# Placing the index chain in TensorE's order, laying the PSUM banks of two layers otherwise, and one square sum on VectorE

## The chip, the cores and the metric

The kernel runs on one core of a Trainium2 chip. The metric is the device time of one execution in microseconds (us). A core has a matrix engine (TensorE, in the profile PE, with its weight loads as PEld), VectorE (DVE), ScalarE (ACT), GpSimd (POOL) and SyncE (SP), which here issues transfers. TensorE writes its results into PSUM, which the kernel uses as eight banks of 128 partitions by 512 fp32 numbers.

## The reference

A decoder trunk of two layers over 512 positions of width 1024, all in fp32. Cut to what matters here:

```python
def rmsnorm(x, g):
    y = x * rsqrt(mean(x * x, axis=-1) + EPS)
    return y * g

def even_layer(x, ...):                      # layer 0
    p = rmsnorm(x, g_norm) @ w_in            # q, k, v, o, z_a, gates, u, z_b
    y_a = mLSTM(conv(q), conv(k), v, gates)  # 4 heads of 256, output gate, head norm, silu gate
    y_b = multi-scale causal pooling of u    # 4 groups, silu gate
    return x + concat(y_a, y_b) @ w_out

def odd_layer(x, ...):                       # layer 1
    p = rmsnorm(x, g_norm) @ w_in            # q, ckv, qi, ki, wi, z
    k, v = rmsnorm(ckv) @ w_uk, rmsnorm(ckv) @ w_uv      # 16 heads of 64, q and k normed
    for each block of 128 queries:
        score = sum over 4 index heads of wi * relu(qi . ki)     # causal
        idx   = top_k(score, 128)                                # min(256, 512 // 4)
        out   = softmax(q . k[idx] / 8 + bias) @ v[idx]
    return x + (out * silu(z)) @ w_out
```

## The kernel before

**Products.** Every fp32 product is done as three fp32r matmuls: an operand is split into a rounded part `h` and a rest `l`, and h*h, h*l and l*h are summed in PSUM. Activations are split by `split` (ScalarE copies `h`, L115; VectorE subtracts, L112). Weights come in tiles of at most 1024 columns (`wtile`): a transfer into `raw`, ScalarE casts `wh` (L147), VectorE or GpSimd subtracts for `wl` (L148). Each of the three has three buffers, so a fourth weight tile waits until the matmuls of the first are done. `dense_tok` (matmuls L180 to L182) gives results with tokens on the partitions, one block `t` of 128 tokens per accumulator; `dense_ch` and `part_ch` (L209 to L211) give channels on the partitions.

**Order.** The work of each stage is written as a string of steps (`ORDER_B`, `ORDER_A` for layer 0, `ORDER` for layer 1), run one after the other; a scheduler then simulates the engines and sets the final order of each engine's instructions by priority and readiness. So an instruction's place on an engine is fixed before the run, and moves when anything near it changes.

**PSUM.** `psum_pools` lays the pools onto the banks in the order of its arguments. Layer 0 has `mm` (4 banks, 0 to 3, dense accumulators) and `bg` (4 banks, 4 to 7, all else). Layer 1 has `mm` (3 banks, 0 to 2), `qk` (2 banks, 3 and 4, query-key products), `tr` (2 banks, 5 and 6, transposes) and `po` (1 bank, 7). `bg()` gives a `tr` bank in layer 1.

**Start.** While x arrives in eight pieces, `arrive(k)` scales it by the norm's gain and `squares(k)` adds its squares to `ssum` (ScalarE squares, GpSimd adds, L251). `norm_factors` sums `ssum` over the channels by four matmuls with one column (L257), VectorE adds epsilon (`n_ss`, L259), GpSimd raises to -1/2 (L260, the factors `r4`), VectorE lays them on a diagonal (L262, `n_dg`), one more matmul spreads them over the partitions (L265), and ScalarE copies this to `r_bc` (L266). `v0_gates` and `tok_v_raw` scale the values of two heads by `r4` (VectorE's `v_l` is L374), `gate_chain` begins (`nf` L387, `lf` L390), and `normalise` makes the normed x: VectorE multiplies (`sq`, L313), ScalarE casts `xn_h` (L314), VectorE and GpSimd in turn subtract for `xn_l` (L315). Then the pooling steps begin with `dense_ch` on it.

**Change of layer.** The output projection of layer 0 ends in `next_x` for each of eight channel blocks: VectorE adds to `xT` (L606), `scaled` makes `xn_h` and `xn_l` (L241, L242), `squares` adds to `ssum`. `norm_factors` follows, then the pools of layer 1 are opened.

**Index stage.** A `dense_tok` with groups of one token block each gives 324 columns of the index projection (qi, ki, wi) in 24 matmuls per block t0 to t3. `ev_idx` scales the block by `r4` on ScalarE (L640 to L642), TensorE transposes it in three pieces (L645) into a `tr` bank, and `split` makes the tiles `aq` and `ak`. Then `scores` (step i, L711 to L718) forms the index scores with `head_pairs` (L679 and L682, into `qk`) and VectorE's L718; `select` (step s) takes the top 128 by rounds of max and match_replace on VectorE (L725, L726); `attend` (step a) does logits (VectorE L832, which writes `st`), the exponential and its scaling on ScalarE (L834, L836), transposes on TensorE (L844) and the products with v (L853 to L855, into `po`), and VectorE multiplies into `zy` (L859). Steps q, k, v, z are projections that fill TensorE between; `head_norm` evacuates q and k (`q_n`, L763, transposed in L767), z's evacuation is L803.

Of the kernel before, what the change touches and what calls it, by code (L numbers as in the profile page):

```python
# [12 lines left out]
ALU = mybir.AluOpType  # L13
# [4 lines left out]
NT = 4  # L18
NK = 8
# [38 lines left out]
def trunk(ctx: ExitStack, tc: tile.TileContext, a: dict, out: bass.AP):  # L58
    nc = tc.nc
    V, A, G, T = nc.vector, nc.scalar, nc.gpsimd, nc.tensor  # L60
# [5 lines left out]
    ps = {}  # L66
    ps_pools = ExitStack()

    def psum_pools(**banks):
        ps_pools.close()  # L70
        ps.clear()
        for n, b in banks.items():
            ps[n] = ps_pools.enter_context(tc.tile_pool(name="ps_" + n, bufs=b, space=PSUM))

    ctx.callback(ps_pools.close)
    psum_pools(mm=4, bg=4)

    def bank(n):
        return ps[n].tile([128, 512], F32, name=n)

    def mm():
        return bank("mm")
    dr = ctx.enter_context(tc.tile_pool(name="dr", bufs=1, space=bass.MemoryType.DRAM))

    def bg():
        return bank("bg" if "bg" in ps else "tr")
# [3 lines left out]
    ident = cst[:, O_IDENT:O_IDENT + 128]  # L90
# [20 lines left out]
    def sub_f32r(dst, src, h):  # L111
        V.tensor_tensor(dst, src, h.bitcast(F32), op=ALU.subtract)  # L112

    def split(h, l, src):
        A.copy(h, src)  # L115
        sub_f32r(l, src, h)
# [17 lines left out]
    def wtile(shape, loads, queue=nc.sync):  # L134
        n = math.prod(shape)
        raw = wp.tile([128, 1024], F32, name="raw", bufs=3)
        wh = wp.tile([128, 1024], F32R, name="wh")
        wl = wp.tile([128, 1024], F32R, name="wl")

        def view(t):  # L140
            t = t[:, :n]
            if len(shape) == 2:
                t = t.rearrange("p (x y) -> p x y", x=shape[0])
            return t
        for sl, src in loads:
            queue.dma_start(view(raw)[:, sl[0], sl[1]], src)
        A.copy(wh[:, :n], raw[:, :n])  # L147
        low_engine[0].tensor_tensor(wl[:, :n], raw[:, :n], wh[:, :n].bitcast(F32), op=ALU.subtract)  # L148
        return view(wh), view(wl)
# [3 lines left out]
    def wrows(w, r0, nk, c0, n):  # L153
        return w[r0:r0 + 128 * nk, c0:c0 + n].rearrange("(k p) c -> p k c", p=128)

    def wcols(cols, kk, queue=nc.sync):
        loads, off = [], 0
        for w, c0, m in cols:
            loads.append(((ALL, slice(off, off + m)), wrows(w, 128 * kk[0], len(kk), c0, m)))
            off += m  # L160
        return wtile([len(kk), off], loads, queue)

    def dense_tok(act, ks, cols, evac, groups=(range(NT),), share=False):

        n = sum(x[2] for x in cols)
        step = min(1024 // n, len(ks))
        ws = {}

        def part(t, k0, ps):
            kk = ks[k0:k0 + step]
            if k0 not in ws:
                ws[k0] = wcols(cols, kk)
            wh, wl = ws[k0]
            for j, k in enumerate(kk):
                ah, al = act(k)
                ts = slice(128 * t, 128 * t + 128)
                first, last = (k0 + j == 0), (k0 + j == len(ks) - 1)
                T.matmul(ps, ah[:, ts], wh[:, j], start=first, stop=False)  # L180
                T.matmul(ps, ah[:, ts], wl[:, j], start=False, stop=False)  # L181
                T.matmul(ps, al[:, ts], wh[:, j], start=False, stop=last)  # L182

        for tts in groups:
            if share:
                two = mm().rearrange("p (u c) -> p u c", u=2)
                for u, t in enumerate(tts):
                    for k0 in range(0, len(ks), step):
                        part(t, k0, two[:, u])
                evac(tts[0], two)  # L190
                continue
            acc = {t: mm() for t in tts}
            for k0 in range(0, len(ks), step):
                for t in tts:
                    part(t, k0, acc[t][:, :n])
                    if k0 + step >= len(ks):
                        evac(t, acc[t])

    def dense_ch(act, w, c0, evac, r0=0):

        ps = mm()
        part_ch(act, wtile([NK, 128], [((ALL, ALL), wrows(w, r0, NK, c0, 128))]), range(NK), ps)
        evac(ps)
# [25 lines left out]
    xn_h = per.tile([128, NK, S], F32R, name="xn_h")  # L229
    xn_l = per.tile([128, NK, S], F32R, name="xn_l")  # L230
    xn = lambda k: (xn_h[:, k], xn_l[:, k])
    ones = nm.tile([128, 128], F32, name="ones")
    V.memset(ones, 1.0)
    ssum = nm.tile([128, S], F32, name="ssum")
# [9 lines left out]
    def squares(k):  # L244

        if k == 0:
            A.activation(ssum, xT[:, k], AF.Square, scale=1.0 / 32)
            return
        sq = nm.tile([128, S], F32, name="sq", bufs=2)
        A.activation(sq, xT[:, k], AF.Square, scale=1.0 / 32)  # L250
        G.tensor_tensor(ssum, ssum, sq, op=ALU.add)  # L251

    def norm_factors():

        p = bg()
        for t in range(NT):
            T.matmul(p[:, t:t + 1], ssum[:, 128 * t:128 * t + 128], ones[:, 0:1], start=True, stop=True)  # L257
        ss = sm.tile([128, NT], F32, name="n_ss")
        V.tensor_scalar(ss, p[:, 0:NT], EPS, None, op0=ALU.add)  # L259
        G.tensor_tensor(r4, ss, mhalf[:, :NT], op=ALU.pow)  # L260
        dg = nm.tile([128, NT, 128], F32, name="n_dg", tag="sq", bufs=2)
        V.tensor_tensor(dg, ident[:, None, :].to_broadcast([128, NT, 128]),  # L262
                        r4[:, :, None].to_broadcast([128, NT, 128]), op=ALU.mult)
        p = bg()
        T.matmul(p, ones, dg.rearrange("p t c -> p (t c)"), start=True, stop=True)  # L265
        A.copy(r_bc, p)  # L266


    warm = nm.tile([128, S], mybir.dt.bfloat16, name="warm")
# [9 lines left out]
    def arrive(k):  # L279
        nc.sync.dma_start(xT[:, k], xv[:, k])  # L280
        if k == 0:
            nc.sync.dma_start(e_g, a["e_norm"])
        scaled(y_h[:, k], y_l[:, k], k, e_g)
        squares(k)

    arrive(0)
    for k in range(NK):
        low_engine[0] = V if k % 2 == 0 else G
        wh, wl = wcols([(a["e_w_in"], 2048, 256), (a["e_w_in"], 5120, 264)], [k], nc.scalar if k < 2 else nc.sync)
        wh, wl = wh[:, 0], wl[:, 0]  # L290
# [9 lines left out]
        for t in range(NT):  # L300
            ts = slice(128 * t, 128 * t + 128)
# [35 lines left out]
    w_in, w_out = a["e_w_in"], a["e_w_out"]  # L337
# [267 lines left out]
    def next_x(c, ps):  # L605
        V.tensor_tensor(xT[:, c], ps, xT[:, c], op=ALU.add)  # L606
        nc.sync.dma_start(x_one[c], xT[:, c])
        scaled(xn_h[:, c], xn_l[:, c], c, o_g)
        squares(c)

    dense_ch4(y, w_out, 0, next_x, lambda c: mm())
    for c in range(4, NK):
        dense_ch(y, w_out, 128 * c, lambda ps: next_x(c, ps))
    norm_factors()
    V.tensor_scalar(r16, r4, 1.0 / 16, None, op0=ALU.mult)

    y_pool.close()

    w_in, w_out = a["o_w_in"], a["o_w_out"]
    w_uk, w_uv = a["o_w_uk"], a["o_w_uv"]  # L620
    psum_pools(mm=3, qk=1, tr=2, po=1)
    GR = ((0, 1), (2, 3))
    p2 = ctx.enter_context(tc.tile_pool(name="p2", bufs=1))
    zy = p2.tile([128, 8, S], F32, name="zy")
# [9 lines left out]
    ki_h, ki_l = (p2.tile([128, S], F32R, name=n, tag=n, bufs=3) for n in ("ak_h", "ak_l"))  # L634
    wi = p1.tile([128, NT, 4], F32, name="wi")

    def ev_idx(t, ps):
        qk = t1.tile([128, 6, 64], F32, name="qk_tok", tag="cb")
        r = r4[:, t:t + 1]
        A.activation(qk[:, 0:5], ps[:, 0:320].rearrange("p (h c) -> p h c", h=5), AF.Copy, scale=r)  # L640
        A.copy(qk[:, 5], qk[:, 4])
        A.activation(wi[:, t], ps[:, 320:324], AF.Copy, scale=r16[:, t:t + 1])  # L642
        p = bg()[:, 0:384].rearrange("p (c t) -> p c t", c=3)
        for c in range(3):
            T.transpose(p[:, c], qk[:, 2 * c:2 * c + 2], ident)  # L645
        ts = slice(128 * t, 128 * t + 128)
        split(qi_h[:, :, ts], qi_l[:, :, ts], p[:, 0:2])
        split(ki_h[:, ts], ki_l[:, ts], p[:, 2])
    low_engine[0] = G
    dense_tok(xn, range(NK), [(w_in, 1280, 324)], ev_idx, [(t,) for t in range(NT)])  # L650


    ckv_h = p1.tile([128, 2, S], F32R, name="ckv_h")
# [261 lines left out]
```

## Time and profile before

Three runs took 760.47, 760.7 and 761.76 us, median 760.7. The profiled execution took 760.41 us, with a span from first to last instruction of 758.6 us and a mean granted TensorE clock of 0.997 of full speed.

| engine | busy us | share of the span |
|---|---|---|
| PE (matmul) | 733.3 | 97% |
| PEld (weight load, beside PE) | 621.4 | 82% |
| DVE | 458.2 | 60% |
| ACT | 383.8 | 51% |
| POOL | 304.2 | 40% |

An engine's busy time counts its instructions alone. "idle before, releaser" is the time an engine stood still ahead of an instruction and the instruction that ended the wait. Times of day are microseconds from the start of the span. The profile shows every engine's rows with their line in the kernel; names are the program's, with buffer numbers left out.

### The profile page before, as it was taken

To read this page: it belongs to the slowest core of one execution; us is meant where nothing else is said; L and a number is where in the kernel's file an instruction comes from. 1 tells how busy PE (TensorE), PEld (TensorE's weight loads), DVE (VectorE), ACT (ScalarE), POOL (GpSimd) and SP (SyncE) were. 2 spreads that over 40 slices of the span, in tenths; PEclk is the share of its full clock that TensorE was granted. 3 is DMA by queue.
4 is the path that set the end of the run, shared out by engine and by line. 5 is a ranking of instruction groups with operands and counts; after the bars stand their busy time and mean duration, and the time that the engine had idled before them with its cause. 6 is when DMAs were issued, how large, how long until landed. Compare 5 with 4: busy or idle time off the path is not lost.

```text
span 758.6 us, 11075 instructions
## 1 busy us (share of the span) xinstructions
PE 733.3 (97%) x4123; PEld 621.4 (82%) x4123; DVE 458.2 (60%) x944; ACT 383.8 (51%) x724; POOL 304.2 (40%) x254
## 2 busy tenths in 40 slices
PE   8989999999999999999999999999999998999987
PEld 6887888887888889888988888988898996777776
DVE  6686533434635866235514573399999986788531
ACT  6445333272535544344633453453565775998710
POOL 5455547723002011031363376246234752753321
PEclk9999999999999999999999999999999999999999
DMA  7623342345231323333322143513331220110061
GB/s 223 166 71 86 84 111 70 111 124 153 83 96 59 91 90 88 92 91 93 84 84 84 56 152 114 140 42 88 94 98 57 65 89 29 57 57 1 13 210 55
DMA packets 83989, 69.19 MB, mean 91 GB/s; under 512 B 3884, under 2 KB 71900, under 8 KB 83936
## 3 DMA queue, kind: packets, MB, share of 16 engines
q1 hardware_dynamic: 82144, 65.83, 30.2%
q10 hardware_dynamic: 1760, 2.66, 1.0%
q8 instruction: 32, 0.52, 0.3%
q14 instruction: 21, 0.17, 0.1%
q0 software_dynamic: 32, 0.01, 0.0%
HBM read 64.25 MB, written 4.23 MB: 90 GB/s over the span
## 4 chain that ended last, share of the span: by engine, by line
PE 79%; DVE 12%; ACT 5%; issue 2%; POOL 1%; DMA 1%; SPq 0%; DVEq 0%; POOLq 0%; ACTq 0%
PE mm L209 13%; PE mm L210 13%; PE mm L211 13%; PE mm L180 7%; PE mm L181 7%; PE mm L182 7%; DVE sel L726 1%; ACT lg L834 1%; DVE m L725 1%; DVE sel L718 1%; DVE pt_l L112 1%; PE qk L209 1%; ACT wh L147 1%; PE qk L211 1%; DVE wl L148 1%
## 5 line engine op out<-in xcount | busy, mean ns | idle before, releaser
L148 POOL TENSOR_TENSOR wl<-raw,wh 128x1024 fp32r<-128x1024 f32 (+4 forms) x65 | 148.5, 2285 | 265.0 <-ACT wh L147 220.8
L147 ACT CAST wh<-raw 128x1024 fp32r<-128x1024 f32 (+4 forms) x117 | 113.5, 972 | 175.5 <-PE mm L210 54.4
L209 PE MATMUL mm<-xn_h,wh 128*128 128x512 f32 x336 | 132.5, 396 | 4.4 <-DVE v_l L374 1.9
L210 PE MATMUL mm<-xn_l,wh 128*128 128x512 f32 x336 | 132.3, 394 | 0.0
L211 PE MATMUL mm<-xn_h,wl 128*128 128x512 f32 x336 | 131.9, 392 | 0.0
L182 PE MATMUL mm<-wh,xn_l 128*128 128x256 f32 (+2 forms) x384 | 123.6, 323 | 0.0
L181 PE MATMUL mm<-wl,xn_h 128*128 128x256 f32 (+2 forms) x384 | 123.5, 322 | 0.0
L180 PE MATMUL mm<-wh,xn_h 128*128 128x256 f32 (+2 forms) x384 | 120.8, 323 | 0.9 <-DVE xT L606 0.9
L148 DVE TENSOR_TENSOR wl<-raw,wh 128x1024 fp32r<-128x1024 f32 (+2 forms) x52 | 65.8, 1266 | 63.0 <-ACT wh L147 62.9
L180 PEld LDWEIGHTS mm<-wh,xn_h 128*128 128x128 f32 x384 | 72.0, 188 | 8.3 <-ACT wh L147 1.3
L209 PEld LDWEIGHTS mm<-xn_h,wh 128*128 128x128 f32 x336 | 63.1, 188 | 18.3 <-DVE v_l L374 2.0
L182 PEld LDWEIGHTS mm<-wh,xn_l 128*128 128x128 f32 x384 | 72.2, 188 | 6.4 <-issue 0.6
L181 PEld LDWEIGHTS mm<-wl,xn_h 128*128 128x128 f32 x384 | 72.2, 188 | 6.3 <-issue 0.5
L210 PEld LDWEIGHTS mm<-xn_l,wh 128*128 128x128 f32 x336 | 63.3, 188 | 14.1 <-issue 0.6
L211 PEld LDWEIGHTS mm<-xn_h,wl 128*128 128x128 f32 x336 | 63.2, 188 | 13.9
L211 PE MATMUL mm<-y_h,wl 128*128 128x512 f32 x128 | 50.2, 394 | 0.4 <-DVE wl L148 0.4
L210 PE MATMUL mm<-y_l,wh 128*128 128x512 f32 x128 | 50.3, 393 | 0.0
L209 PE MATMUL mm<-y_h,wh 128*128 128x512 f32 x128 | 48.8, 394 | 0.9 <-ACT y_h L115 0.9
L515 DVE SCALAR_TENSOR_TENSOR cv<-mm,s_conv,cv 128x511 f32<-128x511 f32 (+2 forms) x48 | 35.8, 746 | 16.2 <-ACT cv L513 15.3
L124 POOL TENSOR_TENSOR q_r<-q_ss,mhalf 128x8 f32<-128x8 f32 x16 | 27.2, 1701 | 40.5 <-DVE q_ss L121 32.7
L834 ACT ACTIVATE lg<-lg,st 128x128 f32<-128x128 f32 (+3 forms) x64 | 35.8, 561 | 9.4 <-DVE st L832 9.3
L836 ACT ACTIVATE lg<-lg,st 128x128 f32<-128x128 f32 (+3 forms) x64 | 34.0, 560 | 4.1 <-DVE st L835 3.9
(274 smaller groups left out, 1529.0 us busy)
## 6 DMA issues: line engine op xcount, KB each, us to landing
raw<-in_e_w_in_dram SPq DMA_DIRECT2D x52, 512.0 KB, 3.8
raw<-in_o_w_in_dram SPq DMA_DIRECT2D x18, 512.0 KB, 3.9
raw<-in_e_w_out_dram SPq DMA_DIRECT2D x16, 512.0 KB, 3.7
raw<-in_o_w_out_dram SPq DMA_DIRECT2D x8, 512.0 KB, 3.5
xT<-in_xT_dram SPq DMA_DIRECT2D x8, 256.0 KB, 3.7
x_one<-xT SPq DMA_DIRECT2D x8, 256.0 KB, 2.7
abias<-lines SPq DMA_DIRECT2D x4, 512.0 KB, 3.9
o_sb<-x_one SPq DMA_DIRECT2D x8, 256.0 KB, 4.0
```

Source lines behind the costliest of these rows:

```text
L124: G.tensor_tensor(dst, ss, mhalf[:, :n], op=ALU.pow)
L147: A.copy(wh[:, :n], raw[:, :n])
L148: low_engine[0].tensor_tensor(wl[:, :n], raw[:, :n], wh[:, :n].bitcast(F32), op=ALU.subtract)
L180: T.matmul(ps, ah[:, ts], wh[:, j], start=first, stop=False)
L181: T.matmul(ps, ah[:, ts], wl[:, j], start=False, stop=False)
L182: T.matmul(ps, al[:, ts], wh[:, j], start=False, stop=last)
L209: T.matmul(ps, wh[:, j], ah, start=(k == 0), stop=False)
L210: T.matmul(ps, wh[:, j], al, start=False, stop=False)
L211: T.matmul(ps, wl[:, j], ah, start=False, stop=(k == NK - 1))
L515: V.scalar_tensor_tensor(u[:, j:], ps[:, :S - j], w[:, 3 - j:4 - j], u[:, j:], op0=ALU.mult, op1=ALU.add)
L834: A.activation(lg[:, :n], lg[:, :n], AF.Exp, scale=-1.0, bias=st[:, 0:1], accum_out=st[:, 1:2])
L836: A.activation(lg[:, :n], lg[:, :n], AF.Copy, scale=st[:, 2:3])
```

## The change

It has four parts.

1. In layer 0 the pool `bg` is laid onto banks 0 to 3 and `mm` onto banks 4 to 7.
2. The last of the eight additions to `ssum` (k = 7), in both layers, is issued on VectorE instead of GpSimd.
3. At the change of layer `psum_pools` is called ahead of `norm_factors`, so that its matmuls write `tr` banks of layer 1; `norm_factors` returns the last of its four sum matmuls.
4. The index projection no longer goes through `dense_tok` but is written out, with three calls per token block (k0 = 0, 3, 6), and `tc.issue_after` puts four of the twelve calls behind a given instruction in TensorE's order: the start of t1 behind the norm sums, the last part of t1 behind the transposes of t0, the middle of t2 behind those of t1, the middle of t3 behind those of t2. The matmuls, evacuations and transposes are the same in number and shape.

```diff
-    psum_pools(mm=4, bg=4)
+    psum_pools(bg=4, mm=4)
...
-        G.tensor_tensor(ssum, ssum, sq, op=ALU.add)
+        (V if k == NK - 1 else G).tensor_tensor(ssum, ssum, sq, op=ALU.add)
...
-            T.matmul(p[:, t:t + 1], ssum[:, 128 * t:128 * t + 128], ones[:, 0:1], start=True, stop=True)
+            sums = T.matmul(p[:, t:t + 1], ssum[:, 128 * t:128 * t + 128], ones[:, 0:1], start=True, stop=True)
...
+        return sums
...
-    norm_factors()
+    psum_pools(mm=3, qk=1, tr=2, po=1)
+    sums = norm_factors()
...
-    psum_pools(mm=3, qk=1, tr=2, po=1)
...
-    def ev_idx(t, ps):
+    idx_acc, idx_tr = {}, {}
+
+    def idx_part(t, k0):
+
+        kk = range(k0, min(k0 + 3, NK))
+        if k0 not in idx_w:
+            idx_w[k0] = wcols([(w_in, 1280, 324)], kk)
+        wh, wl = idx_w[k0]
+        ps, ts = idx_acc[t][:, :324], slice(128 * t, 128 * t + 128)
+        for j, k in enumerate(kk):
+            T.matmul(ps, xn_h[:, k, ts], wh[:, j], start=(k == 0), stop=False)
+            T.matmul(ps, xn_h[:, k, ts], wl[:, j], start=False, stop=False)
+            T.matmul(ps, xn_l[:, k, ts], wh[:, j], start=False, stop=(k == NK - 1))
+
+    def idx_evac(t):
+        ps = idx_acc[t]
...
-            T.transpose(p[:, c], qk[:, 2 * c:2 * c + 2], ident)
+            idx_tr[t] = T.transpose(p[:, c], qk[:, 2 * c:2 * c + 2], ident)
...
-    dense_tok(xn, range(NK), [(w_in, 1280, 324)], ev_idx, [(t,) for t in range(NT)])
+    idx_w = {}
+    for t in range(NT):
+        idx_acc[t] = mm()
+        for k0 in (0, 3, 6):
+            behind = {(1, 0): sums, (1, 6): idx_tr.get(0), (2, 3): idx_tr.get(1), (3, 3): idx_tr.get(2)}.get((t, k0))
+            with tc.issue_after(behind.ins) if behind else ExitStack():
+                idx_part(t, k0)
+        idx_evac(t)
```

Below, rows of an engine's order as the scheduler left it. They hold no times.

**VectorE at the start.** Before, between the value rest `v_l` of accumulator mm_108 and that of mm_441 (a PSUM bank that the first pooling projection takes next):

```order
L374 SCALAR_TENSOR_TENSOR v_l_386<-mm_108,r4_89,v_h_385 128x256
L315 TENSOR_TENSOR xn_l_85<-sq_409,xn_h_84 128x512
L313 SCALAR_TENSOR_TENSOR sq_417<-xT_83,e_g_104,r_bc_91 128x512
L390 SCALAR_TENSOR_TENSOR lf_565<-gt_393,nf_564 128x16
L315 TENSOR_TENSOR xn_l_85<-sq_417,xn_h_84 128x512
L313 SCALAR_TENSOR_TENSOR sq_421<-xT_83,e_g_104,r_bc_91 128x512
L313 SCALAR_TENSOR_TENSOR sq_425<-xT_83,e_g_104,r_bc_91 128x512
L148 TENSOR_TENSOR wl_678<-raw_676,wh_677 128x1024
L313 SCALAR_TENSOR_TENSOR sq_429<-xT_83,e_g_104,r_bc_91 128x512
L315 TENSOR_TENSOR xn_l_85<-sq_425,xn_h_84 128x512
L374 SCALAR_TENSOR_TENSOR v_l_386<-mm_441,r4_89,v_h_385 128x256
```

After, the same place (all lines behind L73 are one or more higher):

```order
L388 SCALAR_TENSOR_TENSOR nf_564<-gt_393 128x16
L316 TENSOR_TENSOR xn_l_85<-sq_409,xn_h_84 128x512
L314 SCALAR_TENSOR_TENSOR sq_417<-xT_83,e_g_104,r_bc_91 128x512
L375 SCALAR_TENSOR_TENSOR v_l_386<-mm_108,r4_89,v_h_385 128x256
L375 SCALAR_TENSOR_TENSOR v_l_386<-mm_441,r4_89,v_h_385 128x256
L391 SCALAR_TENSOR_TENSOR lf_565<-gt_393,nf_564 128x16
L316 TENSOR_TENSOR xn_l_85<-sq_417,xn_h_84 128x512
```

The rest of mm_441 has moved up by nine instructions: it now stands directly behind that of mm_108, and `lf`, the norm products from sq_421 on, the weight rest wl_678 and two `xn_l` come behind it.

**TensorE at the norm sums of layer 1.** Before, they come behind 37 of the index projection's matmuls, into a bank of `bg`:

```order
L182 MATMUL mm<-wh,xn_l 128x324
L180 MATMUL mm<-wh,xn_h 128x324
L257 MATMUL bg<-ones,ssum 128x1 x4
L181 MATMUL mm<-wl,xn_h 128x324
L182 MATMUL mm<-wh,xn_l 128x324
L180 MATMUL mm<-wh,xn_h 128x324
```

After, they come right behind the 24 matmuls of t0, into a bank of `tr`:

```order
L649 MATMUL mm<-wl,xn_h 128x324
L650 MATMUL mm<-wh,xn_l 128x324
L257 MATMUL tr<-ones,ssum 128x1 x4
L648 MATMUL mm<-wh,xn_h 128x324
L649 MATMUL mm<-wl,xn_h 128x324
L650 MATMUL mm<-wh,xn_l 128x324
```

The first transposes, which before form a group of six near the end of the stage, form a group of three in the middle of t1's matmuls, behind the spreading matmul:

```order
L649 MATMUL mm<-wl,xn_h 128x324
L650 MATMUL mm<-wh,xn_l 128x324
L265 MATMUL tr<-n_dg,ones 128x512
L661 MATMUL tr<-cst,qk_tok 128x128 x3
L648 MATMUL mm<-wh,xn_h 128x324
L649 MATMUL mm<-wl,xn_h 128x324
```

The twelve transposes stand in groups of 6, 1 and 5 before, and of 3, 3, 2, 1, 2 and 1 after.

**TensorE late in the attention.** Before, between the query-key products qk_5677 (384 keys) and qk_5730 (512 keys) stand 23 other rows, 15 of them matmuls of a q projection (accumulator mm_6543); the last of these rows:

```order
L844 MATMUL tr_5650<-cst_72,lg_5643 128x128
L181 MATMUL mm_6543<-wl_6564,xn_h_84 128x256
L182 MATMUL mm_6543<-wh_6563,xn_l_85 128x256
L853 MATMUL po_5565<-pt_h_5569,av_h_4715 128x256
L854 MATMUL po_5565<-pt_h_5569,av_l_4716 128x256
L855 MATMUL po_5565<-pt_l_5570,av_h_4715 128x256
L679 MATMUL qk_5730<-ak_h_4533,aq_h_4317 128x512
```

After, mm_6543 is done 14 rows ahead of qk_5677, and two products with v are what is left between the two:

```order
L869 MATMUL tr_5595<-cst_72,lg_5580 128x128
L869 MATMUL tr_5595<-cst_72,lg_5588 128x128
L704 MATMUL qk_5677<-ak_h_4819,aq_h_4885 128x384
L707 MATMUL qk_5677<-ak_h_4819,aq_h_4885 128x384
L707 MATMUL qk_5677<-ak_l_4820,aq_h_4885 128x384 x2
L707 MATMUL qk_5677<-ak_h_4819,aq_l_4886 128x384 x2
L878 MATMUL po_5565<-pt_h_5569,av_h_4715 128x256
L879 MATMUL po_5565<-pt_h_5569,av_l_4716 128x256
L704 MATMUL qk_5730<-ak_h_4533,aq_h_4317 128x512
```

What moved is the filler: the projection's matmuls now stand in front of both query-key products instead of between them.

## Rows read from the trace of the kernel before

**Rows 1.** The page: busy us (share of the span) x instructions, by engine.
```profile
PE 733.3 (97%) x4123; PEld 621.4 (82%) x4123; DVE 458.2 (60%) x944; ACT 383.8 (51%) x724; POOL 304.2 (40%) x254
```

**Rows 2.** TensorE's waits: line waited for, us in total, times, longest us.
```profile
PE qk L679 <- DVE st L832: 1.9, 2, 1.7
PE mm L209 <- DVE v_l L374: 1.9, 1, 1.9
...
PE tr L767 <- DVE q_n L763: 1.1, 1, 1.1
...
PE mm L180 <- DVE xT L606: 0.9, 1, 0.9
...
PE mm L209 <- DVE zy L803: 0.8, 1, 0.8
```

**Rows 3.** Three windows: us, busy (x count) by engine, PEclk, DMA share, GB/s.
```profile
46.00:52.00 6.00, 4.10 (x25) 3.54 (x24) 5.98 (x10) 4.16 (x8) 3.50 (x3) 1.00 0.17 44
466.00:481.00 15.00, 15.00 (x104) 14.51 (x102) 2.60 (x6) 4.29 (x10) 3.16 (x4) 1.00 0.32 88
520.00:540.00 20.00, 18.16 (x100) 15.31 (x99) 19.66 (x49) 7.58 (x12) 9.21 (x6) 1.00 0.30 80
```

**Rows 4.** PE timeline, start: start us, us, instruction [idle before <-releaser].
```profile
27.49 0.95 PE L257 MATMUL bg<-ones,ssum 128*128 128x1 f32 x8
...
49.20 0.50 PE L209 MATMUL mm<-xn_h,wh 128*128 128x512 f32 x1 [1.90 <-DVE v_l L374]
```

**Rows 5.** POOL timeline, start.
```profile
27.97 1.30 POOL L148 TENSOR_TENSOR wl<-raw,wh 128x520 fp32r<-128x520 f32 x1 [2.34 <-ACT wh L147]
29.23 1.02 POOL L260 TENSOR_TENSOR r<-n_ss,mhalf 128x4 f32<-128x4 f32 x1
```

**Rows 6.** DVE timeline, start.
```profile
43.02 0.69 DVE L315 TENSOR_TENSOR xn_l<-sq,xn_h 128x512 fp32r<-128x512 f32 x1 [0.60 <-ACT xn_h L314]
...
48.67 1.25 DVE L374 SCALAR_TENSOR_TENSOR v_l<-mm,r,v_h 128x256 fp32r<-128x256 f32 x3
```

**Rows 7.** PE timeline, change of layer and index stage.
```profile
464.47 0.39 PE L180 MATMUL mm<-wh,xn_h 128*128 128x324 f32 x1 [0.88 <-DVE xT L606]
...
470.02 0.95 PE L257 MATMUL bg<-ones,ssum 128*128 128x1 f32 x8
...
480.37 0.82 PE L645 MATMUL tr<-cst,qk_tok 128*128 128x128 f32 x6
...
481.18 0.28 PE L180 MATMUL mm<-wh,xn_h 128*128 128x256 f32 x1
```

**Rows 8.** DVE timeline, the same stage.
```profile
463.64 0.69 DVE L606 TENSOR_TENSOR xT<-mm,xT 128x512 f32<-128x512 f32 x1 [1.80 <-PE mm L211]
465.12 1.22 DVE L242 SCALAR_TENSOR_TENSOR xn_l<-xT,o_g,xn_h 128x512 fp32r<-128x512 f32 x1 [0.79 <-ACT xn_h L241]
...
489.38 0.48 DVE L718 SCALAR_TENSOR_TENSOR sel<-relu,wi,sel 128x256 f32<-128x256 f32 x1
```

**Rows 9.** POOL timeline, the same stage.
```profile
465.75 1.74 POOL L251 TENSOR_TENSOR ssum<-ssum,sq 128x512 f32<-128x512 f32 x1
471.25 1.02 POOL L260 TENSOR_TENSOR r<-n_ss,mhalf 128x4 f32<-128x4 f32 x1 [3.76 <-DVE n_ss L259]
```

**Rows 10.** ACT timeline, the same stage.
```profile
472.30 0.97 ACT L640 ACTIVATE qk_tok<-mm,r 128x320 f32<-128x320 f32 x2 [6.69 <-POOL r L260]
...
478.49 1.05 ACT L147 CAST wh<-raw 128x1024 fp32r<-128x1024 f32 x1 [0.89 <-PE mm L182]
```

**Rows 11.** PE timeline, late in the attention.
```profile
624.02 0.50 PE L679 MATMUL qk<-ak_h,aq_h 64*128 64x512 f32 x1
...
627.44 0.65 PE L679 MATMUL qk<-ak_h,aq_h 64*128 64x512 f32 x1 [1.73 <-DVE st L832]
```

**Rows 12.** A window behind that wait, columns as in Rows 3.
```profile
628.00:630.00 2.00, 2.00 (x12) 1.35 (x8) 1.92 (x9) 1.08 (x4) 0.28 (x1) 0.50 0.28 47
```

## The prediction

> **What bounds the kernel now.** I read the busy times first. TensorE is busy for 733.3 of 758.6 us, and VectorE, next, for 458.2 [rows 1]. So TensorE sets the time, and its instructions are the same in number and shape after the change: only its roughly 25 us of idle time (758.6 - 733.3) and the switches between kinds of matmul can move. I then read the list of TensorE's waits, to see which of them touch lines of the diff [rows 2]: 1.9 us for `v_l` at the start, 0.9 us for `xT` at the change of layer, 1.1 us for `q_n` and 0.8 us for `zy` where VectorE is late, and 1.9 us for `st` in the attention. Next the windows around these places show who is short there: at 46 to 52 us VectorE is busy for 5.98 of 6.00 us and TensorE for 4.10; at 466 to 481 us TensorE is busy throughout, and all others have room; at 520 to 540 us VectorE has 19.66 of 20.00 us, and TensorE lacks 1.84 [rows 3]. The timelines of each engine at these places come last.
>
> **Start of layer 0.** TensorE waits 1.90 us, until 49.20, for the rest `v_l` of an accumulator whose bank the pooling projection takes [rows 2, 4]. VectorE forms it at 48.67, behind a series of norm products and a weight rest [rows 6]. The accumulator was done long before; only VectorE's order made it late. In the new order, seven instructions stand behind it that stood in front: three `sq` and two `xn_l` of about 0.7 us each (0.69 for an `xn_l` [rows 6]), `lf`, and a weight rest. That is 3.5 us in norm work alone, so `v_l` comes before 46 us, and the bank is free when TensorE gets there at 47.30. Why the order moved is not that the factors come sooner: the sums go from 27.49 to just ahead of the k = 5 matmuls, but the power on GpSimd stays at 29.23, since it stands behind the weight rest of 27.97 [rows 4, 5]. What is late next is the normed x itself, as the seven instructions are what the next projection reads. It takes its eight pieces in turn, three matmuls each, so the pieces pushed back are wanted later than the first. If one is still late, part of the wait returns. Bounds: gain 1.9 to 0; I take 1.7, nearer to the full wait because it ended on that one instruction. Laying `mm` and `bg` otherwise moves no work in layer 0 itself.
>
> **Change of layer.** The first index matmul starts at 464.47 after 0.88 us of waiting for VectorE's last addition to `xT`, 463.64 to 464.33 [rows 7, 8]. Its data don't need that addition, for it begins with k = 0; its bank does, since `mm` of layer 1 lies on the banks from which the addition reads. With layer 0's accumulators on banks 4 to 7 the index accumulators have banks of `bg`, long free. So this wait goes: gain 0.88, bounds 0 (a weight tile or the k = 7 piece late instead: `xn_l` of it ends at 465.12 + 1.22 = 466.34 [rows 8], and the k = 7 matmuls begin 21 matmuls behind 463.59, at 466.7, so it is in time by 0.4 us) and 0.88.
>
> **Norm sums and the chain behind them.** Before, the last addition to `ssum` is GpSimd's, 465.75 to 467.49 [rows 9]; the sums run at 470.02 [rows 7], the power at 471.25 and ends at 472.27 [rows 9], the first evacuation follows at 472.30 [rows 10]. After, VectorE adds right behind `xn_l` at 466.34 in about 0.69 us (the addition of the same shape [rows 8]), ending at 467.03. The sums stand behind 24 matmuls from 463.59 at 0.15 us each (37 matmuls from 464.47 to 470.02 [rows 7]), at 467.2: 2.8 us earlier, and with them the power, at 469.4, and the first evacuation. The moved work itself costs TensorE nothing: the same four one-column matmuls, now ahead of others. VectorE's extra 0.69 us lies in a stretch where it is busy for 2.60 of 15 us [rows 3]. The transposes of t0 no longer stand near the end of the stage at 480.37 but around 473; so the tiles `aq` and `ak` are complete sooner, and VectorE's first score, at 489.38 [rows 8], comes some 5 us earlier (I take 3 to 6: t3's transposes still end the stage).
>
> **What the fixed places cost.** First, switches. The group of six transposes moved the next matmul kind by 481.18 - 480.37 = 0.81 us, with one index matmul in it, so 0.66 us without it; six alone at pitch 0.15 would be 0.9, so such a group costs no more than matmuls, but each change of kind shows a longer row. Going from three groups to six I price at 0.15 us for each new group (one pitch), 0.45, say 0.5; bounds 0 and 1. Second, waits. A group fixed in TensorE's order waits for its evacuation on ScalarE (0.97 us for two blocks [rows 10]), and all later matmuls wait behind it, where the scheduler before left the transposes until all was ready. t0's evacuation ends near 470.5 and its transposes stand 27 matmuls behind the sums, so at 467.2 + 0.8 + 27 x 0.15 = 472.1: a margin of 1.6 us, little for the smaller groups. And t3's index matmuls now end later, while they hold the weight tiles: the next tile's cast at 478.49 already waited 0.89 us for such matmuls [rows 10]. The stretch has no idle time now [rows 3], so it can only lose: 0 to 1.5, I take 0.6.
>
> **Behind it, where VectorE is short.** At 520 to 540 us TensorE loses 1.84 us to VectorE's late `q_n` and `zy` [rows 2, 3]. The selection on VectorE started at 489.38 [rows 8], and a start some 5 us sooner shortens the line in front of both. But the steps of the order are the same, and VectorE is full throughout the stretch, so a new filler in front can take part of it: gain 0 to 1.84, I take 1.0, a little over half.
>
> **Late in the attention.** Here the scheduler has moved filler, as the third pair of orders shows. Before, query-key products of 512 keys start at 624.02, and the next at 627.44 after 1.73 us for `st` [rows 11]; between qk_5677 and qk_5730 the filler made any wait unnecessary. After, qk_5730 has two short products in front and may wait as that one did, 1.73 us; in exchange, the filler now covers what is ahead of qk_5677, and VectorE and ScalarE come to this place earlier. I take 0; bounds a loss of 4.5 (below) and a gain of 2, about the whole `st` wait of 1.9 [rows 2].
>
> **The sum**, in the profiled execution's time of 760.41 us (its span is 758.6): -1.7 - 0.88 + 0.5 + 0.6 - 1.0 + 0 = -2.48, so 757.9. The median of the runs shown is 0.29 above the profiled one: 758.2 us.
>
> **Rivals.** (1) *More is won.* All waits named go (1.9 + 0.88 + 1.84), switches cost 0.5 and stalls 0.2, and the earlier VectorE also takes the late `st` wait and the lower clock behind it, 2: -5.9, so 754.5 + 0.29 = 754.8. For it: all these waits end on VectorE. Against: the filler is gone where the `st` wait is. (2) *Given back.* The start's 1.7 us returns because a norm piece is late in the wait's place: 758.2 + 1.7 = 759.9. For it: VectorE is busy for 5.98 of 6.00 us there [rows 3], so the delay may only change its name. Against: the pieces are wanted one after another. (3) *Slower: the late filler.* qk_5730 and qk_5784 both wait for `st` with hardly anything in front, 2 x 1.73 = 3.46. In the trace such a wait is followed by a low clock: 0.50 of full speed (1.2 GHz) at 628 to 630 [rows 12], two microseconds doing the work of one, so 1.0 more. Together 4.46: 758.2 + 4.5 = 762.7. For it: the order itself; against: a sooner VectorE, and that the same filler in front leaves more time for the chain ahead. It decides once the late stretch loses over 4.0 us, as 758.2 + 4.0 is 762.2.
>
> The Trainium skill bears on this rival (TensorE: Matmul & The Clock Gate, Part 4: PE-mode transpose): transposes don't count as busy for the clock the way matmuls do. By that rule the transposes that follow qk_5730 could hold the low clock, by my estimate for another 1.0 us, and this rival would come to 763.7. The trace speaks neither way: at 466 to 481 the clock stays at 1.00 with six transposes among matmuls [rows 3], and at 628 to 630, with four of them, the wait had come before [rows 12]. Neither the sum nor a chance above rests on it.
>
> **How the numbers follow.** The forecast has 0.48, its own range 756.6 to 759.2 (its terms off by about half together); more won 0.16; given back 0.20; slower 0.16. A run of this kernel can tell about 0.2% or 1.5 us: under 759.2 is faster, over 762.2 slower. So faster has 0.48 + 0.16 = 0.64, no change 0.20, slower 0.16. The range reaches from the first rival's time, 754.8, to the third's, 762.7: it leaves out half of the first rival (0.08) and half of the third (0.08).
>
> **What would show it.** At the start, no wait of L209's matmuls on `v_l`, or one on `xn_h` or `xn_l` in its place (rival 2). At the change of layer, the first index matmul within 0.2 us of the last output matmul, sums near 467, the power before 470. In the index stage, idle time of TensorE ahead of the transposes or of the first weight tile behind it, under 1 us in sum. VectorE's first score near 484, and `q_n` and `zy` waits under 1 us together. Late, the sum of waits on `st` near 2 us; 3.5 or more, with a clock near 0.50 behind, is rival 3. The forecast is wrong if the start's wait stays, if the index stage loses over 1.5 us, or if the late stretch moves by more than 2.

## The result and the profile after

The changed kernel takes 766.75 us (median of four runs, 765.45 to 767.33) against 761.23 us for the kernel before on the same chip (four runs, 760.47 to 761.77): ratio 1.0071, 95% interval 1.0052 to 1.0089. It is slower by 0.7%, where 758.2 us was forecast. Its profiled execution took 767.33 us with a span of 765.6 us, 7.0 more than before. This execution is the slowest of its four and the profiled one of before (760.41 us) faster than all of its own, so the 7.0 us taken apart below stand for 5.5 between the medians.

The busy line of the page, and TensorE's list of waits (line waited for, us in total, times, longest us), answering to [rows 1, 2]:

```profile
PE 736.8 (96%) x4123; PEld 622.4 (81%) x4123; DVE 464.9 (61%) x946; ACT 384.7 (50%) x724; POOL 301.2 (39%) x252
```
```profile
PE po L878 <- DVE zy L884: 4.1, 6, 1.6
PE tr L695 <- DVE c_n L691: 3.0, 1, 3.0
PE tr L792 <- DVE q_n L788: 2.1, 2, 1.2
...
PE qk L704 <- DVE st L857: 1.2, 3, 0.5
...
PE mm L180 <- DVE v_l L375: 0.6, 1, 0.6
PE bg L405 <- DVE a_tok L402: 0.4, 1, 0.4
```

Both waits that the diff reached for are gone: 1.9 us in front of L209 at the start, and 0.9 us for `xT`. A new one of 3.0 us stands in their place, for `c_n` (L691), the normed compressed keys and values in `ev_ckv`, a function that the diff does not touch. VectorE's timeline has it (start us, us, instruction, idle before):

```profile
487.68 2.34 DVE L743 SCALAR_TENSOR_TENSOR sel<-relu,wi,sel 128x256 f32<-128x256 f32 x1 [0.60 <-ACT relu L742]
...
495.92 2.79 DVE L743 SCALAR_TENSOR_TENSOR sel<-relu,wi,sel 128x384 f32<-128x384 f32 x1
...
498.97 0.59 DVE L743 SCALAR_TENSOR_TENSOR sel<-relu,wi,sel 128x384 f32<-128x384 f32 x1
...
502.31 2.27 DVE L743 SCALAR_TENSOR_TENSOR sel<-relu,wi,sel 128x384 f32<-128x384 f32 x1
...
506.87 0.87 DVE L691 SCALAR_TENSOR_TENSOR c_n<-mm,c_r,b_o_g_kv 128x256 f32<-128x256 f32 x2
```

The same instruction, a score addition on 384 columns, takes 0.59 us at 498.97 and 2.79 or 2.27 us at two other times. GpSimd's timeline of the same stretch says what is different:

```profile
487.35 2.40 POOL L148 TENSOR_TENSOR wl<-raw,wh 128x1024 fp32r<-128x1024 f32 x1 [13.25 <-ACT qk_tok L657]
...
495.90 2.40 POOL L148 TENSOR_TENSOR wl<-raw,wh 128x1024 fp32r<-128x1024 f32 x1 [1.06 <-ACT wh L147]
...
501.77 2.39 POOL L148 TENSOR_TENSOR wl<-raw,wh 128x1024 fp32r<-128x1024 f32 x1
504.12 0.51 POOL L689 TENSOR_TENSOR c_r<-c_r,r 128x2 f32<-128x2 f32 x1
```

Each long addition starts inside one of GpSimd's weight rests and ends 0.3 to 0.4 us after it. The kernel before has such meetings too, but shorter ones, and `c_n` comes sooner (VectorE, then GpSimd, then TensorE's first transpose of `c_n`):

```profile
495.50 1.61 DVE L718 SCALAR_TENSOR_TENSOR sel<-relu,wi,sel 128x384 f32<-128x384 f32 x1
...
500.72 1.29 DVE L718 SCALAR_TENSOR_TENSOR sel<-relu,wi,sel 128x384 f32<-128x384 f32 x1
...
502.86 0.86 DVE L666 SCALAR_TENSOR_TENSOR c_n<-mm,c_r,b_o_g_kv 128x256 f32<-128x256 f32 x2
```
```profile
494.30 2.39 POOL L148 TENSOR_TENSOR wl<-raw,wh 128x1024 fp32r<-128x1024 f32 x1 [1.47 <-ACT wh L147]
...
499.18 2.41 POOL L148 TENSOR_TENSOR wl<-raw,wh 128x1024 fp32r<-128x1024 f32 x1
```
```profile
504.56 0.27 PE L670 MATMUL tr<-cst,c_n 128*128 128x128 f32 x1
```

Against 0.48 us for an addition of 256 columns and 0.60 for one of 384, the additions in front of `c_n` lose 1.0 + 0.7 = 1.7 us before and 1.86 + 2.19 + 1.67 = 5.7 us after: 4.0 more. `c_n` starts 506.87 - 502.86 = 4.0 us later. Without these losses it would come near 501.2 in both kernels, although VectorE begins its additions 2.8 us sooner after (486.60 against 489.38 [rows 8]): eight rounds of max and match_replace instead of six now stand in front of `c_n`, and VectorE waits 0.60 + 0.45 + 0.45 us for ScalarE's `relu`. TensorE, which before came to its transposes at 504.56 without a wait, now waits, and two windows show the clock behind it (columns as in [rows 3]):

```profile
507.49 0.30 PE L695 MATMUL tr<-cst,c_n 128*128 128x128 f32 x1 [3.00 <-DVE c_n L691]
```
```profile
506.00:508.00 2.00, 0.51 (x5) 0.54 (x6) 1.97 (x7) 0.60 (x1) 0.00 (x0) 1.00 0.67 196
508.00:510.00 2.00, 2.00 (x13) 1.68 (x13) 1.97 (x6) 0.59 (x1) 0.00 (x0) 0.60 0.00 0
510.00:512.00 2.00, 2.00 (x12) 1.35 (x9) 1.97 (x7) 1.08 (x3) 0.00 (x0) 0.54 0.00 0
512.00:514.00 2.00, 2.00 (x19) 2.00 (x19) 1.93 (x7) 0.73 (x3) 0.19 (x1) 1.00 0.00 0
```

Four microseconds at 0.60 and 0.54 lose 2 x 0.40 + 2 x 0.46 = 1.7 us, mostly at the 1.2 GHz level. Wait and clock make 4.7 us; TensorE falls back by 4.75 us from matmul 2520 to 2610.

Where the 7.0 us of the span lie, worked out from the time at which the n-th matmul record starts in each trace (after less before, at stage borders):

| stage (n) | us then | change in it | forecast |
|---|---|---|---|
| start (to 360) | -0.05 | -0.05 | -1.7 |
| rest of layer 0 (to 2160) | +0.24 | +0.29 | 0 |
| change of layer, sums (to 2280) | -0.99 | -1.23 | -0.88 |
| index stage (to 2520) | +0.61 | +1.60 | +1.1 |
| selection, first projections (to 2970) | +5.72 | +5.11 | -1.0 |
| attention, output | +7.0 | +1.3 | 0 |

### The profile page after: what moved, and what is told of

It reads as the page before. It is cut to its first block, busy times and chain, and to the rows that moved or that the text cites. A ratio compares the mean times of both kernels' runs of the same rounds, so it can differ in the third digit from the quotient of the medians.

```text
span 765.6 us, 11068 instructions
## 1 busy us (share of the span) xinstructions
PE 736.8 (96%) x4123; PEld 622.4 (81%) x4123; DVE 464.9 (61%) x946; ACT 384.7 (50%) x724; POOL 301.2 (39%) x252
## 4 chain that ended last, share of the span: by engine, by line
PE 76%; DVE 12%; ACT 7%; issue 2%; DMA 1%; SPq 1%; POOL 0%; DVEq 0%; ACTq 0%
PE mm L209 13%; PE mm L211 13%; PE mm L210 13%; PE mm L180 7%; PE mm L181 7%; PE mm L182 7%; ACT lg L859 2%; DVE sel L743 2%; DVE sel L751 1%; DVE wl L148 1%; DVE m L750 1%; ACT lg L861 1%; ACT wh L147 1%; PE tr L869 1%; PE po L880 1%
## 5 line engine op out<-in xcount | busy, mean ns | idle before, releaser
L209 PE MATMUL mm<-xn_h,wh 128*128 128x512 f32 x336 | 132.1, 395 | 1.8 <-ACT xn_h L115 1.1
L181 PE MATMUL mm<-wl,xn_h 128*128 128x256 f32 (+1 forms) x352 | 113.8, 324 | 0.4 <-DVE wl L148 0.4
L182 PE MATMUL mm<-wh,xn_l 128*128 128x256 f32 (+1 forms) x352 | 113.1, 322 | 0.0
L180 PE MATMUL mm<-wh,xn_h 128*128 128x256 f32 (+1 forms) x352 | 111.2, 324 | 0.3 <-ACT wh L147 0.3
L209 PEld LDWEIGHTS mm<-xn_h,wh 128*128 128x128 f32 x336 | 63.0, 188 | 15.6 <-ACT xn_h L115 1.3
L181 PEld LDWEIGHTS mm<-wl,xn_h 128*128 128x128 f32 x352 | 66.5, 189 | 7.3 <-issue 0.9
L180 PEld LDWEIGHTS mm<-wh,xn_h 128*128 128x128 f32 x352 | 66.1, 189 | 7.4 <-issue 0.9
L182 PEld LDWEIGHTS mm<-wh,xn_l 128*128 128x128 f32 x352 | 66.6, 189 | 5.9
L209 PE MATMUL mm<-y_h,wh 128*128 128x512 f32 x128 | 48.8, 394 | 0.9 <-ACT y_h L115 0.9
```

The lines of the kernel that those rows point to most:

```text
L209: T.matmul(ps, wh[:, j], ah, start=(k == 0), stop=False)
```

## The experiments

The theory (called M, meeting, in the expectations): a score addition on VectorE stands still while GpSimd forms a weight rest, the changed order makes them meet in front of `c_n`, and `c_n` holds TensorE. Rivals: the fixed places cost the time themselves (P), VectorE's square sum (S), the bank layout (B), plain load on VectorE (D). Ratios are to the kernel before in runs of the same chip, with 95% intervals; all experiments were timed but the first, and each compared with its own runs of before (medians 761.7 to 762.0 us).

**m1_port: the meeting by itself.** A small kernel in place of the trunk; VectorE's series runs twice, the second time beside this:

```diff
+    for _ in range(18):
+        G.tensor_tensor(wl, raw, wh.bitcast(F32), op=ALU.subtract)
```

> A kernel that leaves out the whole trunk: VectorE runs a series of five kinds of instruction on 384 columns once alone and once while GpSimd runs 18 subtractions of 1024 columns (like the weight rests) back to back. Theory M (meeting): score additions (scalar_tensor_tensor on two SBUF tiles) stand still until a GpSimd subtraction ends, so they take about 0.6 us alone and up to 2.8 us beside GpSimd, while max and match_replace stay at their 0.55 us. Rival D (VectorE's own load, no meeting): every kind takes the same in both halves, within 0.1 us.

Rows of its VectorE timeline, alone (first five) and beside GpSimd, whose 18 subtractions run from 17.63 for 44.96 us:

```profile
8.71 0.61 DVE L44 SCALAR_TENSOR_TENSOR sel<-relu,wi,sel 128x384 f32<-128x384 f32 x1
9.24 0.55 DVE L46 TENSOR_TENSOR l<-relu,wh 128x384 fp32r<-128x384 f32 x1
...
10.70 0.61 DVE L48 SCALAR_TENSOR_TENSOR cn<-ps,wi,relu 128x384 f32<-128x384 f32 x1
...
14.27 0.34 DVE L53 COPY cn<-relu 128x384 f32<-128x384 f32 x1
...
15.87 0.55 DVE L50 MAX8 m<-big 128x8 f32<-128x384 f32 x1
...
18.41 2.69 DVE L44 SCALAR_TENSOR_TENSOR sel<-relu,wi,sel 128x384 f32<-128x384 f32 x1
21.02 2.69 DVE L46 TENSOR_TENSOR l<-relu,wh 128x384 fp32r<-128x384 f32 x1
...
27.30 0.60 DVE L48 SCALAR_TENSOR_TENSOR cn<-ps,wi,relu 128x384 f32<-128x384 f32 x1
27.83 0.54 DVE L50 MAX8 m<-big 128x8 f32<-128x384 f32 x1
...
28.88 0.53 DVE L51 MATCH_REPLACE8 big<-m,big 128x384 f32<-128x384 f32 x1
...
33.98 2.03 DVE L53 COPY cn<-relu 128x384 f32<-128x384 f32 x1
```

As M expected: an addition or subtraction that reads two SBUF tiles takes 2.69 instead of 0.61 or 0.55 us, that is, it gets one turn per GpSimd instruction (44.96 / 18 = 2.50 us each, hardly more than the 2.40 of the trace). The same instruction with one input in PSUM, max and match_replace keep their times. A copy from SBUF to SBUF waits too (0.34 to 2.03), which was not asked for. The Trainium skill has the rule (SBUF — State Buffer, Who interferes with whom): VectorE and GpSimd share one pair of SBUF ports, a VectorE instruction with two SBUF inputs contends for it with a GpSimd instruction that reads SBUF, and whoever issues first keeps it for the whole instruction. These rows agree.

**e5_dve_rests: two of GpSimd's rests in that stretch go to VectorE.**

```diff
-i3 s10 q0 z0
+i3 s10 Q0 z0
```

> The changed kernel with step q0 of the order as Q0: the two weight rests of the first q projection go to VectorE (1.23 us each) instead of GpSimd (2.4 us each). Theory M: the score additions that took 2.34 and 2.79 us in the changed kernel go back to 0.5 to 0.6, c_n comes some 2 us sooner, the 3.0 us wait for it falls under 1.5 and the low clock behind it goes: 3 to 5 us faster than the changed kernel, 762 to 764. Rival P (the fixed places themselves cost the time): c_n is as late, or later with 2.5 us more on VectorE: 766 to 769.

Measured 763.37 us, ratio 1.0019 (1.0008 to 1.0031); the changed kernel has 1.0071. Of the additions in front of `c_n` one remains long (2.73 us, against a rest that stayed on GpSimd), the wait for `c_n` is gone, and TensorE is 4.65 us ahead of the changed kernel at matmul 2610 (0.71 behind before, against 5.36). M, not P. Some of it is lost 60 us later, where a wait for `q_n` has 2.7 us.

**e3_noplace and e2_vsum: without the places, and the square sum alone.**

```diff
-            with tc.issue_after(behind.ins) if behind else ExitStack():
-                idx_part(t, k0)
+            idx_part(t, k0)
```

> The changed kernel without the four fixed places (issue_after left out; banks, VectorE sum and the written-out projection stay). Rival P: the loss goes with the places, 759 to 761. Theory M: VectorE's and GpSimd's order around c_n is the same as in the changed kernel (four score additions and a weight rest in front of it), so most of the loss stays: a wait for c_n of 1.5 us or more, 764 to 767.

```diff
-        G.tensor_tensor(ssum, ssum, sq, op=ALU.add)
+        (V if k == NK - 1 else G).tensor_tensor(ssum, ssum, sq, op=ALU.add)
```

> The kernel before with the last square sum on VectorE alone. If that part costs by itself (rival S: the addition stands in front of a weight rest at 24 us, TensorE waits 0.6 us there), the start is 0.5 us later up to the wait that ended at 49.20 and that wait goes as in the changed kernel: start within 0.3 us of before. Theory M: behind it the index stage is that of before, so c_n meets as little as before: 760 to 762.

e3 took 764.65 us, ratio 1.0036 (1.0022 to 1.0049), in M's range but not by M's place: the wait for `c_n` is 0.5 us, and waits for `q_n` (longest 2.8) and `pt_l` (1.7) came instead. So the fixed places do bring the `c_n` wait, and P is right about half of the loss; the other half comes without them. Its longest wait for `q_n` lies at 518.75, and a meeting stands in front of that one as well: `q_ss`, an instruction on 128x8 that takes 0.14 us at 511.60, takes 1.85 us at 514.03, inside a GpSimd rest that runs from 513.43 for 2.41 us. e2 took 763.74 us, 1.0023 (1.0012 to 1.0034), slower than I expected: its start is 0.28 us sooner at 50.9 us and 0.48 later at 71, but the new order has a wait of 2.4 us for `q_n` near 570. The two additions on another engine changed VectorE's order 100 us behind the second of them.

**e7_no_bank_swap and e4_place_only: the other parts undone.**

```diff
-    psum_pools(bg=4, mm=4)
+    psum_pools(mm=4, bg=4)
```

> The changed kernel with layer 0's PSUM pools laid as before (mm on banks 0 to 3). TensorE's order is the same as in the changed kernel, row for row. Theory M: only the wait for xT at the change of layer comes back (0.9 us), the wait for c_n of about 3 us stays: 0 to 1.5 us slower than the changed kernel, 766 to 769. Rival B (the bank layout brings the loss, by another place of the accumulators): 761 to 763.

```diff
-    psum_pools(bg=4, mm=4)
+    psum_pools(mm=4, bg=4)
...
-        (V if k == NK - 1 else G).tensor_tensor(ssum, ssum, sq, op=ALU.add)
+        G.tensor_tensor(ssum, ssum, sq, op=ALU.add)
```

> The fixed places and the earlier opening of layer 1's pools alone: banks and the last square sum as before. VectorE's and GpSimd's order around c_n is that of the changed kernel. Theory M: the wait for c_n of 2 us or more and the low clock behind it stay, and both the start's 1.9 us for v_l and the 0.9 us for xT are back: 765 to 769. Rival S (VectorE's square sum is the loss): 760 to 762.

e7: 766.92 us, 1.0071 (1.0056 to 1.0087). e4: 769.97 us, 1.0096 (1.0077 to 1.0116). TensorE's waits in e7, and then in e4:

```profile
PE tr L695 <- DVE c_n L691: 3.0, 1, 3.0
...
PE mm L648 <- DVE xT L607: 0.9, 1, 0.9
```
```profile
PE tr L695 <- DVE c_n L691: 2.5, 1, 2.5
...
PE mm L209 <- DVE v_l L375: 2.0, 1, 2.0
...
PE mm L648 <- DVE xT L607: 0.9, 1, 0.9
```

Neither the banks nor the square sum carry the loss at `c_n` (B and S fall; what the sum costs alone, e2 has): `c_n` waits in both, and e4 is even 1 us above what was expected; its start is 2.4 us later than that of before (reason below). The `xT` wait returns with the old banks, as forecast, and in e4 the wait for `v_l` with the sum back on GpSimd. The 0.9 us of e7 does not show in its ratio, whose interval is 2.4 us wide.

**e8_pieces: the same rests, still on GpSimd, in four pieces.** For step q0 alone:

```diff
+        m = n // pieces[0]
+        for c in range(0, n, m):
+            cs = slice(c, c + m)
+            low_engine[0].tensor_tensor(wl[:, cs], raw[:, cs], wh[:, cs].bitcast(F32), op=ALU.subtract)
```

> The changed kernel with the weight rests of step q0 still on GpSimd but cut into four subtractions of 256 columns each. VectorE's order around c_n is that of the changed kernel but for one row. Theory M: a score addition that meets such a rest waits for one piece, not for 2.4 us: those of 128x256 and 128x384 take at most 1.4 us, c_n comes 2 us or more sooner, its wait is under 1.5 us, and the time is 2 to 5 us under the changed kernel: 762 to 765. Rival D (GpSimd's work as such delays VectorE): the additions take as long in sum, 766 to 768.

Measured 761.5 us, ratio 0.9997 (0.9986 to 1.0008): all of the loss is gone. Additions and `c_n` in its VectorE timeline, then GpSimd's rests and the first transpose:

```profile
487.25 0.69 DVE L748 SCALAR_TENSOR_TENSOR sel<-relu,wi,sel 128x256 f32<-128x256 f32 x1 [0.60 <-ACT relu L747]
...
494.02 0.61 DVE L748 SCALAR_TENSOR_TENSOR sel<-relu,wi,sel 128x384 f32<-128x384 f32 x1
...
500.34 1.76 DVE L748 SCALAR_TENSOR_TENSOR sel<-relu,wi,sel 128x384 f32<-128x384 f32 x1
...
503.34 0.86 DVE L696 SCALAR_TENSOR_TENSOR c_n<-mm,c_r,b_o_g_kv 128x256 f32<-128x256 f32 x2
```
```profile
486.92 3.49 POOL L153 TENSOR_TENSOR wl<-raw,wh 128x256 fp32r<-128x256 f32 x4 [13.25 <-ACT wh L149]
...
495.45 2.81 POOL L153 TENSOR_TENSOR wl<-raw,wh 128x256 fp32r<-128x256 f32 x4 [2.46 <-ACT wh L149]
...
498.90 2.78 POOL L153 TENSOR_TENSOR wl<-raw,wh 128x1024 fp32r<-128x1024 f32 x1
```
```profile
504.36 0.27 PE L700 MATMUL tr<-cst,c_n 128*128 128x128 f32 x1
```

The addition that meets the first cut rest takes 0.69 us, where 2.34 stood, and the two behind it, inside the same rest, take 0.48 each. The one that had 2.79 us starts 1.9 us sooner, at 494.02, and is done before the second cut rest begins at 495.45; it takes 0.61. The one at 500.34 meets a rest that is not cut (z0's), so that one exceeded the 1.4 us expected. The price is on GpSimd: a cut rest takes 2.81 to 3.49 us instead of 2.40. `c_n` is 3.5 us sooner than in the changed kernel and nothing waits for it.

**e1_banks: the bank layout alone.**

```diff
-    psum_pools(mm=4, bg=4)
+    psum_pools(bg=4, mm=4)
```

> The kernel before with the bank layout of layer 0 alone. The scheduler's order then has the norm sums and their spreading ahead of the first index matmul, since the index accumulators get the banks that the sums use. Theory: TensorE waits there for the last square sum (GpSimd ends it at 467.5 in the kernel before) and again for the power and the diagonal, 6 to 8 us in all, with a low clock behind: 767 to 771. Rival: the layout alone takes the 0.9 us wait away and costs nothing, 759 to 761.

Measured 773.0 us, 1.0143 (1.0123 to 1.0164). The norm sums in it, ahead of the first index matmul:

```profile
469.51 1.87 PE L257 MATMUL bg<-ones,ssum 128*128 128x1 f32 x8 [3.89 <-POOL ssum L251]
...
473.55 2.04 PE L265 MATMUL bg<-n_dg,ones 128*128 128x512 f32 x2 [2.17 <-DVE r L615]
```

That is 3.9 + 2.2 = 6.1 us of waits, as the theory had it; the stage (matmuls 2160 to 2280) is 10.9 us longer, and the low clock around the waits (0.60 on average from 466 to 480) has most of the other 4.8 us, more than I allowed for. The layout removes one wait and sets a bigger one, unless the sums leave those banks, which the change's early opening of layer 1's pools does.

**f1, f2, f3, f4: does the cut help by itself, and what beats both?** f1 is the kernel before with e8's cut. f2 is e8 with

```diff
-Z1 K1 Q1 s12
+Z1 K1 q1 s12
```

and q1's rests cut as well; f3 has z1 for Z1 too, with rests of z0 and z1 cut (layer 0 has steps of the same names, so theirs are cut too); f4 is the kernel before with f2's cuts and q1, without any of the change.

> The kernel before, with the weight rests of step q0 cut into four subtractions on GpSimd, nothing else. If the cut itself is what e8_pieces won by, whatever the order in front, it wins here too. Theory M: before, the additions in front of c_n lost only 1.0 and 0.7 us to GpSimd and no wait for c_n followed, so there is little to win: within 1.5 us of before, 760 to 763. Rival (the cut is worth 5 us anywhere): 756 to 758.

> e8_pieces with step Q1 as q1, its rests in four pieces too: two weight rests of 1.22 us leave VectorE, which is full from 490 to 600 us, for GpSimd. Theory M: in pieces they cost VectorE little there (max and match_replace don't wait for GpSimd), so the wait for q_n at 567 (1.46 us) goes: 1 to 2 us under e8_pieces. Rival (GpSimd's slower rests, 2.4 us against 1.2, come too late for the matmuls): a wait for wl of over 1 us in its place, no gain or slower by 1 to 2 us.

> f2_q1_pieces with step Z1 as z1 and the rests of z0 and z1 in pieces as well: two more rests leave VectorE. Theory M: another 1 to 2 us from the waits for q_n and zy at 510 to 560, under f2 by 0 to 2 us. Rival as for f2: the rests come late, 0 to 2 us slower than f2.

> The kernel before with the cut rests of f2_q1_pieces (q0 and q1 on GpSimd, four pieces each), but with none of the change. Theory M: the change itself is worth about 1 us once the meetings are gone (the start's and the xT wait less the index stage's cost), so this kernel is 0.5 to 2 us slower than f2_q1_pieces, 760 to 761.5 where before takes 761.8. Rival (the change is worth nothing, all of f2's gain is in the cut rests): the same as f2 within 0.5 us, 759.5.

| kernel | us | ratio to before | 95% |
|---|---|---|---|
| f1, before with q0 cut | 761.62 | 1.0001 | 0.9990 to 1.0012 |
| f2, changed with q0 and q1 cut | 759.53 | 0.9972 | 0.9962 to 0.9983 |
| f3, f2 with z0 and z1 | 757.58 | 0.9945 | 0.9930 to 0.9959 |
| f4, before with q0 and q1 cut | 762.42 | 1.0004 | 0.9992 to 1.0016 |

The cut is worth nothing in the kernel before (f1, f4), 0.7% in the changed kernel (e8), and with q1 it makes the changed kernel 0.3% faster than before. f4 is a little above its expected 761.5. f2 less f4 is 0.0032 of the time, 2.4 us, with intervals that do not touch: that is what the change is worth once the additions don't meet the rests. In the two profiled executions most of it lies at the start: at matmul 360 f4 is 2.27 us behind the kernel before, and f2 is 0.60 ahead. f3 is the fastest of all, 2.0 us under f2 in the medians and 1.2 in the profiled executions; of the 1.2 us, 0.4 are there at matmul 2160, in layer 0, and the rest comes in the selection, by matmul 2970.

## Why the prediction was wrong

**The step that failed** is "Behind it, where VectorE is short": a sooner start of the selection was to shorten VectorE's line, "gain 0 to 1.84, I take 1.0". It cost 5.1 us (matmuls 2520 to 2970), nearly all of it at `c_n`. The bounds shut out a loss without a reason: that VectorE's instructions keep their durations when they move was taken for granted. The head start itself was 2.8 us and was used up ahead of `c_n` by other work, as the argument had allowed. The trace of before held the warning, additions of 1.61 and 1.29 us beside others of 0.60, with a GpSimd rest over each, but the argument read VectorE's busy share there (19.66 of 20 us [rows 3]) as work, and part of such a share is standing still. m1, e5 and e8 show the mechanism from three sides; e4 and e7 that it goes with the order and not with banks or the sum. The rival that had the kernel slower put the loss at the late filler, where 1.3 us of it lie, so it was not right either.

**The other steps.** *Start:* the wait for `v_l` went as said, and the move by seven instructions was right (of the nine rows between the two `v_l`, two now stand in front of both). But against the trace of before the gain was 0.05 us here and 0.3 us on average over the eight profiled kernels that share the sum on VectorE, not 1.7. TensorE comes to the first pooling matmul at 48.56, only 0.64 sooner than 49.20 [rows 4], since it waits 0.60 us for another `v_l` at 43.17, and later 0.43 us for `a_tok`; the wait was paid in parts. Against other kernels with the old wait the gain is larger, by the clock. The same window in before and in f4, whose order in layer 0 is that of before and whose wait was 2.15 us (columns as in [rows 3]):

```profile
50.00:55.00 5.00, 5.00 (x23) 4.13 (x22) 4.97 (x10) 1.36 (x3) 3.69 (x3) 1.00 0.14 27
```
```profile
50.00:55.00 5.00, 5.00 (x15) 4.00 (x16) 5.00 (x11) 2.07 (x3) 3.69 (x3) 0.67 0.09 27
```

In f4, e4 and e1 the granted clock is 0.67, 0.66 and 0.76 there, and they are 2.3, 2.4 and 1.4 us behind before at matmul 360. So the start is worth 0.3 us where the clock stays up behind the wait, as in before and f1, and 1.7 to 2.7 where it falls; the 1.7 of the sum had the wait alone, so that it meets the lower end of the second is luck.

*Change of layer:* right; the first index matmul starts at 463.67, 0.23 us behind the last output matmul at 463.44, and e7 shows the 0.9 us coming back. *Norm sums:* right, at 467.34 (467.2 said) with the power at 468.64. *First score:* 486.60 instead of 489.38 [rows 8], 2.8 us sooner, just under the 3 to 6 that were taken. *Fixed places:* 1.6 us instead of 1.1, inside the bounds of its two parts (0 to 1 and 0 to 1.5). *Late stage:* the trace has +1.3 us for 0 said; the wait of the query-key products for `st` fell to 1.2 us, and the longest wait for `zy` rose from 0.9 to 1.6. A part of the loss is not the order's: e7 has TensorE's order row for row, and there the stretch from matmul 3330 to 3420 costs 0.5 us against 1.7 here. Why layer 0 ends 0.24 us later here and 0.12 sooner in e7 was not tried.

Of rival 1's gain of 5.9 us, f2 has 2.3 and f3 4.2, and both need the rests cut. What stays open is the wait for `q_n` around 570, which e2 and e5 have with 2.4 and 2.7 us, e3 with 1.3 and before not at all: VectorE's new order puts weight rests and max rounds in front of it, and f2, which takes two rests out, leaves 0.7 us; it was not tried by itself.

## What to carry to other kernels

Where VectorE is the second limit, compare the durations of one kind of instruction over the stretch before pricing a move: rows of 1.3 to 2.8 us among rows of 0.6 were meetings with GpSimd here, and each new order dealt them anew. Keep GpSimd's two-input work short per instruction wherever VectorE has two-input work on SBUF near a deadline; cutting each into four cost nothing in the kernel before and gave 0.7% in the changed one. And change an order only with its neighbours in view: each of three parts here moved waits hundreds of instructions away.

## What the runs showed of the hardware that was not expected

A VectorE instruction of tiny size waits as long as a large one: `q_ss` on 128x8, 0.15 us elsewhere, took 1.88 us in the changed kernel, inside a rest of GpSimd that ran from 517.58 for 2.41 us:

```profile
518.15 1.88 DVE L121 TENSOR_SCALAR q_ss<-q_ss 128x8 f32<-128x8 f32 x1
```

And TensorE's clock does not fall behind every such wait. In the late attention, with the same instructions in the same order, this is the row behind a wait in the changed kernel, then in e7:

```profile
636.24 0.35 PE L878 MATMUL po<-pt_h,av_h 128*128 128x256 f32 x1 [1.57 <-DVE zy L884]
```
```profile
637.16 0.35 PE L878 MATMUL po<-pt_h,av_h 128*128 128x256 f32 x1 [1.59 <-DVE zy L884]
```

The granted clock was 0.53 at 638 to 640 and 0.62 at 640 to 642 in the first and 1.00 throughout in the second, which is worth up to 2 x 0.47 + 2 x 0.38 = 1.7 us of work; TensorE comes out of the stretch with 1.2 us more lost (1.7 against 0.5, above), so such a wait cost 1.6 us once and about 2.8 the other time. Behind e5's wait of 2.71 us for `q_n` the clock stayed at 1.00 as well, where it fell to 0.60 behind the 3.0 us for `c_n`.
